# A gated-linear-attention layer: query-times-state products in plain fp32, a backward state kept decayed, gates computed in two halves

## The chip, the core and the metric

The program runs on one core of one Trainium2 chip. A core has five engines with a queue of their own each: TensorE (PE; its weight loads are shown apart as PEld), VectorE (DVE), ScalarE (ACT), GpSimd (POOL) and SyncE (SP), which here issues every DMA. Each engine takes its instructions in the order in which the program holds them, so one that waits holds up what stands behind it on its engine. The metric is the device time of one execution in microseconds (us); lower is better.

## What is computed

One layer of a transformer trunk over 2048 latent tokens and 256 context tokens: a modulated norm, a bidirectional gated linear attention (GLA), a residual, and a SwiGLU feed-forward part (FFN). What matters here is the scan. Per head, with a decay `g` for each channel and token, a state `s` (128 x 256) runs over the tokens:

```
def step(s, inp):
    qc, kc, vc, gc = inp
    b = cumsum(gc, axis=1);  b_end = b[:, -1]
    q_dec = qc * exp(b)
    scores = where(causal, q_dec @ (kc * exp(-b)).T, 0)
    o = scores @ vc + q_dec @ s
    s = exp(b_end) * s + (kc * exp(b_end - b)).T @ vc

o_f = scan(q, k, v, g_f);  o_b = flip(scan(flip(q), flip(k), flip(v), flip(g_b)))
y = (head_rms_norm(o_f + o_b) * silu(r)) @ w_out          # then residual, norm, FFN
g = log_sigmoid(glr @ w_gate + b_gate) / 16
```

The context tokens are scanned first, and their last states start both scans of the latent tokens.

## The kernel before

The latent tokens are worked in 4 groups of 512 tokens (`g`), each of 4 chunks of 128 tokens (`c`; 16 chunks in all, `gc`). There are three stages in time.

**First stage** (to about 820 us). For each group a list of 24 units (`proj_units`) projects k, v with the gate inputs (`proj_vg`, `proj_v`), q and r. Between the units the main loop puts the four steps `s0` to `s3` of each chunk (`gla_stages`), from unit 16 of a group into the next group's units; the last group's chunks lie closer. All matmuls of the projections, and most of GLA, are split: an fp32 operand becomes a high and a low part in the format fp32r (`split`: a cast, and a subtraction on DVE), and `mm3` makes high x high, high x low and low x high, three matmuls in place of one.
- `s0` loads k, q, v of a chunk. For every second chunk it also computes the gates of the pair, in both directions (`gates(0, cp)`, then `gates(1, cp)`): 4 small matmuls each (`pre`), three activations for each half on ACT (L342 to L344), a subtraction (L345, `gcs`) and a running sum (L347, `cs`) for each half on DVE, a middle value (L350) and one pass over the whole (L351).
- `s1` forms the decayed keys `ek` and queries `eq`, and splits v.
- `s2` makes the scores `sc`, the transposed keys `kt`, and the splits. For the forward state it takes `Tf` times the decay `fz`, split into `shi` (ACT, L418) and `slo` (DVE, L419), and the split of the query (`qhi`, `qlo`).
- `s3` makes the state's increments `U` for both directions. The forward one is added into `Tf` (L441); the backward one is copied out (L446) and stored to DRAM as `ub_d`. Then `o` = scores times v (one `mm3`) plus query times state (a second `mm3`), stored as `op_d`.

`proj_vg` leaves the gate inputs in PSUM; DVE takes them out in small steps (`gs` L291 and L292, `glt` L293 to L295) before PE may use that PSUM buffer again.

**Second stage** (about 820 to 1112 us). The chunks are gone through backwards (`back`), five steps each, software-pipelined over neighbouring chunks. `b0` loads `ub`, the decayed backward query `qb`, `op` and r. POOL multiplies `qb` by the chunk's decay `fb` (L650), ACT and DVE split the state `Tb` (`shi`, `slo`) and the query (`qhi`, `qlo`), and DVE updates the state, `Tb` = `Tb` x `fb` + `ub` (L653). `b1` makes query times state with `mm3` and adds it to `op` (L670), then squares on ACT, a power on POOL (`rh`, L82) and a scaling on DVE (`on`, L676). `b2` transposes and multiplies by silu(r) (`rt`, `ohi`, `olo`), `b3` multiplies by the output weights (`py`, 48 matmuls), `b4` scales (`ry` on POOL, L724 on DVE), adds the residual on POOL (L726, `y`), stores it (L727) and normalises it. SP issues the stores and the loads of later chunks in one queue.

**Third stage** (from about 1112 us). The FFN, in a seven-product scheme of split matmuls (L924, L1047). The change does not touch it.

The code's order is not the engines' order: when the program is built, a scheduler places the instructions on each engine by what it expects to be ready. Buffers are pools with a fixed count (`bufs`); a tile that takes a buffer again waits for the last reader.

Of the kernel before, what the change touches and what calls it, by code (L numbers as in the profile page):

```python
# [7 lines left out]
F32 = mybir.dt.float32  # L8
# [26 lines left out]
def trunk(ctx, tc, x, cx, modw, cols, rows, consts, wqkr, wv, wvg, wgate, wout, w1, w2, out):  # L35
# [271 lines left out]
    pair = {}  # L307

    def gla_stages(g, i, c, first):
# [3 lines left out]

        def gtile(shape, name):
            return psg.tile(shape, F32, name=name, tag="ga", bufs=4)

        def s0():
# [10 lines left out]
            e["cs"] = [t[:, c % 2:2 * H:2, :] for t in pair["cs"]]  # L328
            e["lnDf"] = pair["lnDf"][:, c % 2]

        def gates(z, cp):
            flat = lambda t: t.rearrange("p n t -> p (n t)")
            cs = gp.tile([128, 2 * H, 129], F32, name=f"cs{z}", tag=f"cs{z}", bufs=1)
            for hh in range(2):
                pre = gtile([128, 2, 256], "pre")
                for h2 in range(2):
                    h = 2 * hh + h2
                    nc.tensor.matmul(out=pre[:, h2, :], lhsT=wg[z][:, 128 * h:128 * h + 128],
                                     rhs=glrS[i][:, 256 * cp:256 * cp + 256], start=True, stop=True)
                pre = pre.rearrange("p h (c t) -> p (h c) t", c=2)  # L340
                ab = gp.tile([128, 4, 128], F32, name="ab", tag="ab", bufs=2)
                nc.scalar.activation(out=ab, in_=pre, func=AF.Abs)  # L342
                nc.scalar.activation(out=ab, in_=ab, func=AF.Exp, scale=-1.0)
                nc.scalar.activation(out=ab, in_=ab, func=AF.Ln, bias=1.0)  # L344
                nc.vector.scalar_tensor_tensor(out=gcs[:, :, 1:129], in0=pre, scalar=0.0, in1=ab,  # L345
                                               op0=ALU.min, op1=ALU.subtract)
                nc.vector.tensor_tensor_scan(out=flat(cs[:, 4 * hh:4 * hh + 4, :]), data0=flat(rst), data1=flat(gcs),  # L347
                                             initial=0.0, op0=ALU.mult, op1=ALU.add)
            mid = gp.tile([128, 2 * H, 1], F32, name="mid", tag="mid", bufs=2)
            nc.vector.tensor_scalar_mul(out=mid, in0=cs[:, :, 64:65], scalar1=1.0 / 16)  # L350
            nc.vector.scalar_tensor_tensor(out=cs, in0=cs, scalar=1.0 / 16, in1=mid.to_broadcast([128, 2 * H, 129]),  # L351
                                           op0=ALU.mult, op1=ALU.subtract)
            lnD = (pair["lnDf"] if z == 0 else lnDb[:, gc:gc + 2]).rearrange("p c h j -> p h c j")
            nc.gpsimd.tensor_copy(out=lnD[:, :, :, z], in_=mid.rearrange("p (h c) o -> p h (c o)", c=2))
            nc.gpsimd.tensor_copy(out=lnD[:, :, :, 1 - z], in_=cs[:, :, 128:129].rearrange("p (h c) o -> p h (c o)", c=2))
            return cs

        def s1():
            e["ks"], e["qs"] = [], []
            for z in range(2):  # L360
# [14 lines left out]
                if z == 0:  # L375
                    if prev["lnDf"] is not None:
                        fz = gp.tile([128, H], F32, name="fz", tag="fz", bufs=2)
                        nc.vector.tensor_add(out=fz, in0=prev["lnDf"][:, :, 1], in1=lnD[:, :, 0])
                        nc.scalar.activation(out=fz, in_=fz, func=AF.Exp)
                        e["fz"] = fz  # L380
                    prev["lnDf"] = lnD
            e["vhi"] = gp.tile([128, D], F32R, name="vhi", tag="vhi", bufs=1)
# [3 lines left out]
        def s2():  # L386
# [19 lines left out]
            if not is_ctx:  # L406
# [756 lines left out]
```

## Time and profile before

| | |
|---|---|
| median of 3 runs | 2427.31 us (2424.38 to 2429.68) |
| the profiled execution | 2426.05 us |
| its span | 2424.3 us |
| PE busy | 2313.9 us (95%) |
| DVE, ACT, POOL busy | 1644.8, 1083.0, 220.2 us |
| mean granted clock of TensorE | 0.978 |

The span runs from the first to the last instruction of the one profiled execution. A busy PE has a matmul in flight; the granted clock tells at which share of full speed it runs, and it takes two levels, 1.00 (2.4 GHz) and 0.50 (1.2 GHz). Time can thus be lost in two ways on PE: idle before an instruction, and half speed for some microseconds after.

### The profile page before, as it was taken

Reading aid. Unit: us, or ns where it says so; the run is one execution under the profiler, and the core shown is the slowest. Engines: PE = TensorE matmul, PEld = TensorE weight load, DVE = VectorE, ACT = ScalarE, POOL = GpSimd, SP = SyncE. Lnnn points to the kernel's source line nnn. Section 1 sums busy time; section 2 is a strip of 40 time slices with the busy share of each in tenths; the row PEclk is TensorE's granted clock in tenths of the full one; section 3 lists DMA queues with packets and bytes.
Section 4 is the critical chain, followed back from the end, with each engine's and each line's share of the span. In section 5 each row is a group of like instructions: output and inputs, shape, how many; then the busy total and the mean of one; then the engine's idle time right before and its main releaser. Section 6 shows DMA issues by size and latency. Waiting matters only on the chain.

```text
span 2424.3 us, 32896 instructions
## 1 busy us (share of the span) xinstructions
PE 2313.9 (95%) x11686; PEld 1952.2 (81%) x11686; DVE 1644.8 (68%) x2628; ACT 1083.0 (45%) x1930; POOL 220.2 (9%) x290
## 2 busy tenths in 40 slices
PE   8999999999999899787899999999999989999998
PEld 4898898898898777676788888888888868888887
DVE  6756668667669788776777766776565647567554
ACT  3524535435546454434433333543333326555552
POOL 1100001001001144652000000000000000001001
PEclk9999999999999999998999999999999989999999
DMA  8755367476455676657878523543233238559655
GB/s 301 230 197 176 130 211 263 159 230 205 140 199 186 218 243 228 207 190 265 276 255 268 178 96 111 191 137 109 92 109 105 92 113 293 193 184 325 212 182 175
DMA packets 229193, 465.07 MB, mean 192 GB/s; under 512 B 22562, under 2 KB 66210, under 8 KB 229028
## 3 DMA queue, kind: packets, MB, share of 16 engines
q1 hardware_dynamic: 229028, 462.96, 56.5%
q8 instruction: 92, 1.51, 0.3%
q14 instruction: 73, 0.60, 0.1%
HBM read 331.79 MB, written 131.08 MB: 191 GB/s over the span
## 4 chain that ended last, share of the span: by engine, by line
PE 52%; DMA 1%; DVE 0%; SPq 0%; ACT 0%; issue 0%; POOLq 0%; POOL 0%; ACTq 0%
PE X L924 19%; PE X L1047 10%; PE Z L924 10%; PE W L1047 7%; PE Y L924 5%; DMA wraw<-w 0%; DMA T<-T_d 0%; DMA T_d<-hf 0%; DVE sa L957 0%; DVE hf L754 0%; DVE y L1028 0%; SPq L879 0%; DVE a L947 0%; DVE bl L754 0%; DVE t L754 0%
## 5 line engine op out<-in xcount | busy, mean ns | idle before, releaser
L924 PE MATMUL X<-T,whl 128*128 128x512 f32 x2112 | 495.7, 390 | 8.2 <-ACT whl L906 7.1
L924 PEld LDWEIGHTS X<-T,whl 128*128 128x128 f32 x2112 | 396.6, 188 | 91.5 <-ACT whl L906 7.5
L924 PE MATMUL Z<-T,whl 128*128 128x512 f32 x1056 | 255.9, 391 | 9.9 <-ACT T L834 9.9
L1047 PE MATMUL X<-wr,ar 128*128 128x512 f32 x1056 | 243.6, 392 | 11.1 <-ACT wr L1011 11.1
L1047 PEld LDWEIGHTS X<-wr,ar 128*128 128x128 f32 x1056 | 200.0, 190 | 53.7 <-ACT wr L1011 11.5
L924 PEld LDWEIGHTS Z<-T,whl 128*128 128x128 f32 x1056 | 199.2, 189 | 52.3 <-ACT T L834 10.3
L86 PE MATMUL pj<-hhi,whi 128*128 128x512 f32 (+1 forms) x544 | 211.4, 390 | 1.8 <-DVE hhi L75 1.1
L87 PE MATMUL pj<-hlo,whi 128*128 128x512 f32 (+1 forms) x544 | 210.7, 388 | 0.0
L88 PE MATMUL pj<-hhi,wlo 128*128 128x512 f32 (+1 forms) x544 | 210.2, 387 | 0.0
L73 ACT CAST whi<-wf 128x1024 fp32r<-128x1024 f32 x104 | 109.1, 1049 | 213.4 <-PE pj L87 77.4
L1001 DVE TENSOR_TENSOR ar<-ar 128x512 fp32r<-128x512 f32 x154 | 106.2, 691 | 136.0 <-ACT ar L1000 135.1
L76 DVE TENSOR_TENSOR wlo<-wf,whi 128x1024 fp32r<-128x1024 f32 x104 | 126.7, 1222 | 83.0 <-ACT whi L73 72.4
L1047 PE MATMUL W<-wr,ar 128*128 128x512 f32 x792 | 180.5, 389 | 0.0
L1047 PEld LDWEIGHTS W<-wr,ar 128*128 128x128 f32 x792 | 148.6, 188 | 30.9
L1000 ACT CAST ar<-ar 128x512 fp32r<-128x512 f32 x154 | 95.4, 621 | 156.0 <-DMA ar<-S_d 103.7
L86 PE MATMUL pj<-whi,hhi 128*128 128x256 f32 x432 | 124.2, 287 | 5.7 <-DVE gs L292 4.9
L924 PE MATMUL Y<-T,whl 128*128 128x512 f32 x528 | 127.7, 390 | 0.0
L87 PE MATMUL pj<-wlo,hhi 128*128 128x256 f32 x432 | 123.3, 285 | 3.1 <-DVE wlo L76 3.1
L88 PE MATMUL pj<-whi,hlo 128*128 128x256 f32 x432 | 122.8, 284 | 0.0
L86 PEld LDWEIGHTS pj<-hhi,whi 128*128 128x128 f32 x544 | 102.9, 190 | 21.2 <-DVE hhi L75 1.3
L87 PEld LDWEIGHTS pj<-hlo,whi 128*128 128x128 f32 x544 | 103.1, 190 | 20.7 <-DVE hlo L76 1.8
L88 PEld LDWEIGHTS pj<-hhi,wlo 128*128 128x128 f32 x544 | 103.0, 189 | 19.6
(237 smaller groups left out, 4528.1 us busy)
## 6 DMA issues: line engine op xcount, KB each, us to landing
ar<-S_d SPq DMA_DIRECT2D x154, 256.0 KB, 2.8
wf<-wqkr SPq DMA_DIRECT2D x68, 512.0 KB, 4.1
wg<-w SPq DMA_DIRECT2D x44, 512.0 KB, 3.7
wu<-w SPq DMA_DIRECT2D x88, 256.0 KB, 2.6
S_d<-sa SPq DMA_DIRECT2D x88, 256.0 KB, 2.0
wr<-W_d SPq DMA_DIRECT2D x88, 256.0 KB, 2.9
wf<-wv SPq DMA_DIRECT2D x36, 512.0 KB, 4.5
wl<-w SPq DMA_DIRECT2D x66, 256.0 KB, 3.7
```

The source lines that it names most:

```text
L73: nc.scalar.copy(out=hi, in_=src)
L76: nc.vector.tensor_sub(out=lo, in0=src, in1=hi.bitcast(F32))
L86: nc.tensor.matmul(out=ps, lhsT=ahi, rhs=bhi, start=start, stop=False)
L87: nc.tensor.matmul(out=ps, lhsT=ahi, rhs=blo, start=False, stop=False)
L88: nc.tensor.matmul(out=ps, lhsT=alo, rhs=bhi, start=False, stop=stop)
L924: nc.tensor.matmul(out=ps, lhsT=w[:, a, ks], rhs=t[:, k, b, :], start=first and k == 0 and n == 0, stop=k == 3 and n == 2, skip_group_chec ...
L1000: nc.scalar.copy(out=t[:, 0, :], in_=raw)
L1001: nc.vector.tensor_sub(out=t[:, 1, :], in0=raw, in1=t[:, 0, :].bitcast(F32))
L1047: nc.tensor.matmul(out=po[j], lhsT=a[:, x, 128 * j:128 * j + 128], rhs=w[:, z, :], start=first and fp == 0 and n == 0, stop=fp == NFP - 1 ...
```

## The change

Three things are changed.
1. Query times state is one plain fp32 matmul per head, in the first stage (`eq` times `ts`, where `ts` is the decayed forward state, written by ACT alone) and in the second (`qb` times `E`). The splits of query and state, and `mm3`, are gone there. `Tf` is now `ts` + `U`, an addition for two heads at once.
2. The second stage keeps the state already decayed: `E` = decayed `Tb`, and the next `E` is `E` x `fb[gc-1]` + `ub`. So that this holds, `ub` is multiplied by `fb[gc-1]` as ACT copies it out of PSUM, one copy for each head; `fb` is computed for each chunk in `s1` in place of once between the stages. POOL's multiplication of `qb` is gone. Chunk 0 needs no `ub`: its backward `U` and the load are left out.
3. The gates of a pair are computed in two calls. The forward half of the second pair of a group comes with chunk 1, and that of the next group's first pair with chunk 3 (for groups 0 and 1); the backward half stays with the pair's first chunk. The last group's first pair is still computed in one go.

```
+    def gates(g, cp, z):
+        d = pairs.setdefault((g, cp), {})
+        if z in d:
+            return
...
+        cs = gp.tile([128, 2 * H, 129], F32, name=f"cs{z}", tag=f"cs{z}", bufs=2)
...
+    def put_fb(gc, ln1):
+        nc.vector.tensor_add(out=fb[:, gc, :], in0=ln1, in1=lnDb[:, gc, :, 0])
+        x = nc.scalar.activation(out=fb[:, gc, :], in_=fb[:, gc, :], func=AF.Exp)
+        last["exp"] = getattr(x, "ins", x)
...
             if c % 2 == 0:
-                pair["lnDf"] = gp.tile([128, 2, H, 2], F32, name="lnDf", tag="lnDf", bufs=2)
-                pair["cs"] = [gates(z, c // 2) for z in range(2)]
...
+                for z in range(2):
+                    gates(g, c // 2, z)
+                pair["now"] = pairs.pop((g, c // 2))
+            elif is_ctx:
+                pass
+            elif c == 1:
+                gates(g, 1, 0)
+            elif g in (0, 1):
+                gates(g + 1, 0, 0)
...
-                e["qhi"] = gp.tile([128, H, 128], F32R, name="qhi", tag="qhi", bufs=1)
-                e["qlo"] = gp.tile([128, H, 128], F32R, name="qlo", tag="qlo", bufs=1)
-                split(e["qs"][0], e["qhi"], e["qlo"], "dve")
-                e["shi"] = gp.tile([128, H, DV], F32R, name="shi", tag="shi", bufs=1)
-                e["slo"] = gp.tile([128, H, DV], F32R, name="slo", tag="slo", bufs=1)
+                e["ts"] = gp.tile([128, H, DV], F32, name="ts", tag="ts", bufs=1)
                 for h in range(H):
-                    f = e["fz"][:, h:h + 1]
-                    nc.scalar.activation(out=e["shi"][:, h, :], in_=Tf[:, h, :], func=AF.Copy, scale=f)
-                    nc.vector.scalar_tensor_tensor(out=e["slo"][:, h, :], in0=Tf[:, h, :], scalar=f,
-                                                   in1=e["shi"][:, h, :].bitcast(F32), op0=ALU.mult, op1=ALU.subtract)
+                    nc.scalar.activation(out=e["ts"][:, h, :], in_=Tf[:, h, :], func=AF.Copy, scale=e["fz"][:, h:h + 1])
...
                 khi, klo = e["kt"][z]
+                if z == 1 and gc == 0:
+                    break
...
+                        elif not is_ctx:
+                            nc.vector.tensor_add(out=Tf[:, hs, :], in0=e["ts"][:, hs, :], in1=U)
...
                     else:
-                        nc.scalar.copy(out=ub[:, hs, :], in_=U)
+                        for h2 in range(2):
+                            h = 2 * hh + h2
+                            nc.scalar.activation(out=ub[:, h, :], in_=U[:, h2, :], func=AF.Copy, scale=fb[:, gc - 1, h:h + 1])
...
-                    mm3(o[:, h2, :], e["qhi"][:, h, :], e["qlo"][:, h, :], e["shi"][:, h, :], e["slo"][:, h, :], False, True)
+                    nc.tensor.matmul(out=o[:, h2, :], lhsT=e["qs"][0][:, h, :], rhs=e["ts"][:, h, :], start=False, stop=True)
...
-            nc.gpsimd.tensor_tensor(out=qb, in0=qb, in1=fb[:, gc, :].unsqueeze(2).to_broadcast([128, H, 128]), op=ALU.mult)
-            split(Tb, shi, slo)
-            for h in range(H):
-                nc.vector.scalar_tensor_tensor(out=Tb[:, h, :], in0=Tb[:, h, :], scalar=fb[:, gc, h:h + 1], in1=ub[:, h, :],
-                                               op0=ALU.mult, op1=ALU.add)
...
-            split(qb, qhi, qlo)
-            e["q"], e["s"] = (qhi, qlo), (shi, slo)
...
+            e["q"], e["s"] = qb, E[0]
+            if gc:
+                nxt = sp.tile([128, H, DV], F32, name="E", tag="E", bufs=3)
+                for h in range(H):
+                    nc.vector.scalar_tensor_tensor(out=nxt[:, h, :], in0=E[0][:, h, :], scalar=fb[:, gc - 1, h:h + 1],
+                                                   in1=ub[:, h, :], op0=ALU.mult, op1=ALU.add)
+                E[0] = nxt
...
-                    mm3(o[:, h2, :], qhi[:, h, :], qlo[:, h, :], shi[:, h, :], slo[:, h, :], True, True)
+                    nc.tensor.matmul(out=o[:, h2, :], lhsT=e["q"][:, h, :], rhs=e["s"][:, h, :], start=True, stop=True)
```

The scheduler makes new orders of it. The first place is DVE at the gate inputs of group 1, when the gates of group 0's second pair are due; before, DVE holds, up to the second `gs`:

```order
L347 SCALAR_TENSOR_TENSOR cs_2854<-rst,gcs 128x516
L378 TENSOR_TENSOR fz<-lnDf 128x4
L76 TENSOR_TENSOR wlo<-wf,whi 128x1024
L345 SCALAR_TENSOR_TENSOR gcs<-pre,ab 128x4x128
L236 COPY stg<-pj 128x256
L347 SCALAR_TENSOR_TENSOR cs_2854<-rst,gcs 128x516
L291 COPY gs<-pj 128x32
L350 TENSOR_SCALAR mid<-cs_2854 128x8
L368 TENSOR_TENSOR ek<-kc,ek 128x512
L351 SCALAR_TENSOR_TENSOR cs_2854<-cs_2854,mid 128x1032
L292 TENSOR_TENSOR gs<-pj,gs 128x32
L291 COPY gs<-pj 128x32
```

Here `cs_2854` is the backward half, and the forward half (the same six instructions) stands just ahead of these rows. In the changed kernel the same place on DVE reads:

```order
L350 TENSOR_TENSOR fb<-lnDb 128x4
L76 TENSOR_TENSOR wlo<-wf,whi 128x1024
L391 TENSOR_TENSOR ek<-kc,ek 128x512
L236 COPY stg<-pj 128x256
L291 COPY gs<-pj 128x32
L394 SCALAR_TENSOR_TENSOR eq<-qc,eq 128x512
L292 TENSOR_TENSOR gs<-pj,gs 128x32
L350 TENSOR_TENSOR fb<-lnDb 128x4
L293 CAST glt_363<-gs 128x32
L294 CAST glt_363<-gs 128x32
L295 TENSOR_TENSOR glt_363<-gs,glt_363 128x32
L291 COPY gs<-pj 128x32
```

Only one half stands ahead of these rows now; no step of the gates is left between or just ahead of the two `gs`, and the other half stands one chunk earlier in the queue.

The second place is POOL in the second stage, over one chunk; before, its queue reads:

```order
L726 TENSOR_TENSOR y_9484<-y_9484,xt_9634 128x1024
L650 TENSOR_TENSOR qb_10093<-qb_10093,fb 128x512
L80 TENSOR_SCALAR mh<-ssh 128x4
L82 TENSOR_TENSOR rh<-mh,nhalf 128x4
L720 TENSOR_TENSOR sst<-ss_9655 128x1
L80 TENSOR_SCALAR my<-sst 128x1
L82 TENSOR_TENSOR ry<-my,nhalf 128x1
L650 TENSOR_TENSOR qb_10239<-qb_10239,fb 128x512
L726 TENSOR_TENSOR y_9654<-y_9654,xt_9804 128x1024
```

The same chunk's piece of the changed kernel on POOL:

```order
L753 TENSOR_TENSOR y_9122<-y_9122,xt_9256 128x1024
L80 TENSOR_SCALAR mh<-ssh 128x4
L82 TENSOR_TENSOR rh<-mh,nhalf 128x4
L747 TENSOR_TENSOR sst<-ss_9277 128x1
L80 TENSOR_SCALAR my<-sst 128x1
L82 TENSOR_TENSOR ry<-my,nhalf 128x1
L753 TENSOR_TENSOR y_9276<-y_9276,xt_9410 128x1024
```

The multiplications of `qb`, which wait for a load, are gone from ahead of `mh` and of `y`; the rest of POOL's work stands as it stood.

## Rows read from the trace of the kernel before

**Rows 1.** Page, part 1: busy us, share of span, instructions.

```profile
PE 2313.9 (95%) x11686; PEld 1952.2 (81%) x11686; DVE 1644.8 (68%) x2628; ACT 1083.0 (45%) x1930; POOL 220.2 (9%) x290
```

**Rows 2.** Windows by stage: us; PE, PEld, DVE, ACT, POOL busy; granted clock; DMA.

```profile
100.00:820.00 720.00, 693.40 (x4356) 625.59 (x4356) 515.70 (x839) 345.78 (x558) 40.67 (x53) 0.98 0.57 190
820.00:1112.00 292.00, 256.78 (x1244) 209.78 (x1243) 219.88 (x372) 131.35 (x305) 135.30 (x151) 0.95 0.66 224
...
1300.00:1981.00 681.00, 681.00 (x3006) 563.88 (x3005) 437.32 (x679) 257.39 (x451) 0.00 (x0) 1.00 0.37 124
```

**Rows 3.** Waits of PE in 100 to 820: us in total, times, longest.

```profile
PE pj L86 <- DVE gs L292: 4.9, 2, 4.4
PE sc L392 <- DVE eq L371: 4.1, 3, 2.7
PE pj L287 <- DVE gs L291: 3.4, 1, 3.4
PE pj L529 <- DVE gs L291: 3.4, 1, 3.4
```

**Rows 4.** Timeline of DVE before the stall that ends at 288.65: start, us.

```profile
284.30 0.68 DVE L345 SCALAR_TENSOR_TENSOR gcs<-pre,ab 128x512 f32<-128x512 f32 x1
...
285.23 1.22 DVE L347 TENSOR_TENSOR_SCAN cs<-rst,gcs 128x516 f32<-128x516 f32 x1
...
287.18 1.23 DVE L351 SCALAR_TENSOR_TENSOR cs<-cs,mid 128x1032 f32<-128x1032 f32 x1
```

**Rows 5.** Windows at the half clock after two stalls, columns as in Rows 2.

```profile
287.70:294.40 6.70, 5.75 (x24) 5.78 (x25) 4.71 (x16) 1.15 (x2) 0.20 (x1) 0.50 0.37 115
...
731.40:741.60 10.20, 7.73 (x33) 7.12 (x34) 10.18 (x23) 5.00 (x10) 2.90 (x3) 0.50 0.21 67
```

**Rows 6.** PE timeline (start, us), and one tile's durations (ns min/median/max).

```profile
219.18 0.28 PE L86 MATMUL U<-vhi,khi 128*128 128x256 f32 x1
219.30 0.28 PE L87 MATMUL U<-vlo,khi 128*128 128x256 f32 x1
...
211.04 1.95 PE L392 MATMUL sc<-eq,ek 128*128 128x128 f32 x16
...
329.50 1.02 PE L520 MATMUL pj<-acc,ones 128*128 128x512 f32 x2
...
L520 PE MATMUL pj<-acc,ones x8: 590/592/697, 329.5 to 549.0; 128*128 128x512 f32 x8
```

**Rows 7.** Groups of instructions: busy us, mean ns; then idle before them.

```profile
L653 DVE SCALAR_TENSOR_TENSOR Tb<-Tb,fb,ub 128x256 f32<-128x256 f32 x64 | 45.3, 755 | 2.5 <-DMA ub<-ub_d 2.4
...
L419 DVE SCALAR_TENSOR_TENSOR slo<-Tf,fz,shi 128x256 fp32r<-128x256 f32 x64 | 28.4, 478 | 0.0
...
L76 DVE TENSOR_TENSOR slo<-Tb,shi 128x1024 fp32r<-128x1024 f32 x16 | 19.5, 1216 | 4.2 <-ACT shi L73 4.2
...
L76 DVE TENSOR_TENSOR qlo<-qb,qhi 128x512 fp32r<-128x512 f32 x16 | 13.1, 822 | 1.6 <-ACT qhi L73 1.6
```

**Rows 8.** Waits of PE in 820 to 1112, columns as in Rows 3.

```profile
PE o L86 <- ACT hf L103: 9.2, 4, 3.6
PE py L86 <- DVE ohi L75: 6.3, 3, 2.4
PE tp L695 <- DVE on L676: 6.3, 4, 3.2
...
PE o L86 <- ACT qhi L73: 2.6, 1, 2.6
```

**Rows 9.** Waits of POOL and SP from 820; POOL and DVE timelines near 950.

```profile
POOL qb L650 <- DMA qb<-qb_d: 67.8, 10, 39.1
...
SPq L727 <- POOL y L726: 71.2, 14, 9.5
...
949.74 1.04 POOL L650 TENSOR_TENSOR qb<-qb,fb 128x512 f32<-128x512 f32 x1 [8.14 <-DMA qb<-qb_d]
...
952.20 1.15 DVE L676 TENSOR_SCALAR on<-op,rh 128x256 f32<-128x256 f32 x4 [3.15 <-POOL rh L82]
```

More of the change, by code (lines that the diff above doesn't have):

```diff
@@ L306, in trunk, with gtile @@
     prev = {"lnDf": None}
-    pair = {}
+    pair, pairs = {}, {}
+    def gtile(shape, name):
+        return psg.tile(shape, F32, name=name, tag="ga", bufs=4)
+    def gates(g, cp, z):
+        d = pairs.setdefault((g, cp), {})
+        if z in d:
+            return
+        i = 1 if g == NG else g % 2
+        gc = NC_ if g == NG else 4 * g + 2 * cp
+        if z == 0:
+            d["lnDf"] = gp.tile([128, 2, H, 2], F32, name="lnDf", tag="lnDf", bufs=3)
+        flat = lambda t: t.rearrange("p n t -> p (n t)")
+        cs = gp.tile([128, 2 * H, 129], F32, name=f"cs{z}", tag=f"cs{z}", bufs=2)
+        for hh in range(2):
+            pre = gtile([128, 2, 256], "pre")
+            for h2 in range(2):
+                h = 2 * hh + h2
+                nc.tensor.matmul(out=pre[:, h2, :], lhsT=wg[z][:, 128 * h:128 * h + 128],
+                                 rhs=glrS[i][:, 256 * cp:256 * cp + 256], start=True, stop=True)
+            pre = pre.rearrange("p h (c t) -> p (h c) t", c=2)
+            ab = gp.tile([128, 4, 128], F32, name="ab", tag="ab", bufs=2)
+            nc.scalar.activation(out=ab, in_=pre, func=AF.Abs)
+            nc.scalar.activation(out=ab, in_=ab, func=AF.Exp, scale=-1.0)
+            nc.scalar.activation(out=ab, in_=ab, func=AF.Ln, bias=1.0)
+            nc.vector.scalar_tensor_tensor(out=gcs[:, :, 1:129], in0=pre, scalar=0.0, in1=ab,
+                                           op0=ALU.min, op1=ALU.subtract)
+            nc.vector.tensor_tensor_scan(out=flat(cs[:, 4 * hh:4 * hh + 4, :]), data0=flat(rst), data1=flat(gcs),
+                                         initial=0.0, op0=ALU.mult, op1=ALU.add)
+        mid = gp.tile([128, 2 * H, 1], F32, name="mid", tag="mid", bufs=2)
+        nc.vector.tensor_scalar_mul(out=mid, in0=cs[:, :, 64:65], scalar1=1.0 / 16)
+        nc.vector.scalar_tensor_tensor(out=cs, in0=cs, scalar=1.0 / 16, in1=mid.to_broadcast([128, 2 * H, 129]),
+                                       op0=ALU.mult, op1=ALU.subtract)
+        lnD = (d["lnDf"] if z == 0 else lnDb[:, gc:gc + 2]).rearrange("p c h j -> p h c j")
+        nc.gpsimd.tensor_copy(out=lnD[:, :, :, z], in_=mid.rearrange("p (h c) o -> p h (c o)", c=2))
+        nc.gpsimd.tensor_copy(out=lnD[:, :, :, 1 - z], in_=cs[:, :, 128:129].rearrange("p (h c) o -> p h (c o)", c=2))
+        d[z] = cs
@@ L309, in gla_stages @@
+    last = {}
+    def put_fb(gc, ln1):
+        nc.vector.tensor_add(out=fb[:, gc, :], in0=ln1, in1=lnDb[:, gc, :, 0])
+        x = nc.scalar.activation(out=fb[:, gc, :], in_=fb[:, gc, :], func=AF.Exp)
+        last["exp"] = getattr(x, "ins", x)
     def gla_stages(g, i, c, first):
@@ L325, in s0 @@
             if c % 2 == 0:
-                pair["lnDf"] = gp.tile([128, 2, H, 2], F32, name="lnDf", tag="lnDf", bufs=2)
-                pair["cs"] = [gates(z, c // 2) for z in range(2)]
[L328 to L356, printed above, removed]
@@ L358, in s1 @@
+                for z in range(2):
[7 more added lines that the diff above has]
+                gates(g + 1, 0, 0)
+            now = pair["now"]
+            e["cs"] = [now[z][:, c % 2:2 * H:2, :] for z in range(2)]
+            e["lnDf"] = now["lnDf"][:, c % 2]
         def s1():
@@ L381, in s1 @@
                     prev["lnDf"] = lnD
+                elif not is_ctx and gc:
+                    put_fb(gc - 1, lnDb[:, gc, :, 1])
+                    if gc == NC_ - 1:
+                        put_fb(gc, lnDb[:, NC_, :, 1])
             e["vhi"] = gp.tile([128, D], F32R, name="vhi", tag="vhi", bufs=1)
@@ L444, in s3 @@
                         nc.scalar.copy(out=Tb[:, hs, :], in_=U)
-                    else:
-                        nc.scalar.copy(out=ub[:, hs, :], in_=U)
+                    elif is_ctx:
+                        nc.scalar.copy(out=ub[:, hs, :], in_=U)
+                    else:
+                        for h2 in range(2):
+                            h = 2 * hh + h2
+                            nc.scalar.activation(out=ub[:, h, :], in_=U[:, h2, :], func=AF.Copy, scale=fb[:, gc - 1, h:h + 1])
                 if z == 1:
@@ L566, in trunk @@
         wait = 0
-        last = g == NG - 1
-        if last:
+        is_last = g == NG - 1
+        if is_last:
             tail = pu[-3:]
@@ L572, in trunk @@
             u()
-            if not last and i + 1 == nq:
+            if not is_last and i + 1 == nq:
                 for c in range(4):
@@ L579, in trunk @@
                 mu.pop(0)()
-            if last:
+            if is_last:
                 if i + 1 >= LAST_AT:
@@ L601, in trunk @@
     p1.close()
-    nc.vector.tensor_add(out=fb[:, 0:NC_ - 1, :], in0=lnDb[:, 1:NC_, :, 1], in1=lnDb[:, 0:NC_ - 1, :, 0])
-    nc.vector.tensor_add(out=fb[:, NC_ - 1, :], in0=lnDb[:, NC_, :, 1], in1=lnDb[:, NC_ - 1, :, 0])
-    fbf = fb.rearrange("p c h -> p (c h)")
-    last_exp = nc.scalar.activation(out=fbf, in_=fbf, func=AF.Exp)
-    last_exp = getattr(last_exp, "ins", last_exp)
+    last_exp = last["exp"]
     p2 = ExitStack()
@@ L622, in load_wo @@
             split(w, *wo[k])
+    E = {}
     def back(gc):
```

19 lines of the change are left out of this document (9 added, 10 removed).

## Prediction

> **What bounds the kernel now.** The page's first part comes first: PE is busy for 95% of the span, and no other engine comes near it [rows 1]. So the kernel is bound by PE, and a change pays only if it makes PE's own work shorter or takes away time in which PE stands still or runs at half speed. The windows by stage tell where such time is [rows 2]. The FFN's long middle has none: PE is busy 681.00 of 681 us at full clock. The first stage idles 720 - 693.4 = 26.6 us, and its granted clock of 0.98 means that some 2% of 720, 14 us, goes to half speed. The second stage is much worse for its length: 292 - 256.8 = 35.2 us idle, and at 0.95 another 5% of 292, 15 us. Together 41 us in the first and 50 us in the second are the most that can be won; between them the stages hold every instruction that the change touches.
>
> Next I read what PE waits for. In the first stage the largest waits are for DVE: for `gs`, the emptying of the gate inputs' PSUM (4.9, 3.4 and 3.4 us), and for `eq` (4.1) [rows 3]. At the stall that ends at 288.65 DVE is not idle; it is working off the gates of a pair: one half takes two L345 at 0.68, two L347 at 1.22, one L351 at 1.23 and a short L350, about 5.1 us, and two halves stand one behind the other with the `gs` among them [rows 4]. Each long stall is followed by a stretch at the lower of TensorE's two levels, 6.7 us behind that one, 10.2 us behind the one near 732 [rows 5]; at half speed half of that is lost, so a stall of 3.4 us costs some 3.4 + 3.4.
>
> **Part 1a, the fp32 products: a cost on PE.** A split product of 128 x 256 is three matmuls that start 0.12 us apart [rows 6], 3 x 0.12 = 0.36 us per head. The trace has no fp32 matmul of 256 columns, but two neighbours. Each shows as two instructions per matmul. The 16 `sc` instructions of 128 columns cover 1.95 us, which with a last one of about 0.28 is (1.95 - 0.28) / 15 = 0.111 us each; of the two `pj` instructions of 512 columns the second begins 1.02 - 0.59 = 0.43 us after the first [rows 6]. In between, 256 columns come to 0.111 + (0.43 - 0.111) x 128 / 384 = 0.217 us, so a product is 2 x 0.217 = 0.434 us, 0.074 more than before. There are 16 chunks x 4 heads = 64 such products in each stage: +4.7 us in each. Bounds: 0.22 per head (the narrower neighbour's price), which is -9 us for each stage, and 0.86 (the wider one's), +32. The value is linear between two rows, so I hold it for good.
>
> The Trainium skill, "FP8 and Floating Point Precision", section TensorE Precision Notes, says that true fp32 takes four passes through the array. Taken as four for three at the split product's own spacing, that is 0.48 us a head, +7.7 us in each stage, an estimate that would put the total 6 us higher; the two neighbours above, measured, are cheaper than that.
>
> Chunk 0's backward `U` goes: 4 heads x 3 matmuls x 0.12 = -1.4 us on PE.
>
> **Part 1b, the splits: a relief of DVE and ACT.** In the first stage each chunk loses four L419 of 0.478 on DVE [rows 7], 1.9 us, besides the two splits of the query; DVE, busy 515.7 of 720 [rows 2], loses at least 64 x 0.478 = 31 us. None of the waits in [rows 3] names these instructions; they only shorten the queue in front of the ones that are named. I count nothing for that by itself beyond 2 us for the small waits left over, and up to 5 as a bound.
>
> In the second stage DVE loses `slo` (19.5 us) and `qlo` (13.1) out of 219.9 [rows 2, 7], ACT the two casts, POOL the 16 multiplications of `qb`. The four updates of the state (L653) stay as they are. Their mean is 755 ns where L419, of the same shape and beside a quiet POOL, takes 478 [rows 7], so they run against something in this stage; with a third engine's work gone some of that should go too, but I put no sum on it.
>
> **Part 2, the decayed state.** POOL no longer waits for the load of `qb`. This is the larger half of the change in the second stage: POOL stood at that load 10 times for 67.8 us in the trace [rows 9], 39.1 of it once before the stage began to turn. Behind it in POOL's queue stand `mh` and `rh`, for which DVE's `on` waits, and `y`, for whose store SP waits 71.2 us, with the loads of the next chunks behind that store [rows 9]. Near 950 it can be followed: POOL gets `qb` after 8.14 us of waiting, only then `rh`, and DVE starts `on` after 3.15 us of idling [rows 9]. PE's waits in the stage are of this kind: for `on`, for `ohi`, for a PSUM buffer that `hf` on ACT holds [rows 8]. What the change moves to `s1` and `s3` (16 tiny adds and exponentials, two copies more per chunk on ACT, busy 345.8 of 720 [rows 2]) lies beside matmuls; if that cover failed it would be under 1 us a chunk.
>
> How much of the second stage's 50 us goes? At least the wait that ends on a removed instruction, `qhi`, 2.6 us [rows 8], and a unit of clock with it: 3 us. At most some 45, all but the wind-up. DVE loses 32.6 of 219.9 us, 15%, and POOL its longest wait, while the chain op, square, power, `on`, transposes, `ohi` and the order L726, L727, loads remain. I take 27, a little over half, nearer to the upper end since most of PE's waits sit behind the two queues that are emptied. Net of the products: -27 + 4.7 = -22.3.
>
> **Part 3, the gates in halves.** By the order, the two `gs` at group 1 have one half of 5.1 us ahead of them in place of two [rows 4]; the same holds at group 2. The stall of 3.4 us at each then shrinks to about nothing, and with it the 6.7 us at half speed: 2 x (3.4 + 3.4) = 13.6, of which I take 12. The wait for `eq` (the longest 2.7 [rows 3], near 397) stands behind the first gates of group 1, of which one half is gone: 3 with its clock. The stall near 732 is group 3's first pair, which is still computed in one go, and DVE's order there is the same as before: 4.4 us of wait and 10.2 us at half speed [rows 3, 5] stay. The half that is moved needs 5.1 us of DVE somewhere else, six times in all; I put it at nothing, since DVE is idle for 204 of the 720 us [rows 2] and gets 31 us freer, and since PE there works from loaded weights. If it were not covered it would make a stall of up to 3.4 us at each of the six, +20 us.
>
> **The sum.** First stage: +4.7 - 1.4 - 2 - 12 - 3 = -13.7. Second: -22.3. Together -36.0 against the profiled execution's 2426.05, so 2390.0 us. That execution lies 1.3 us under the median of the runs, less than the runs differ among themselves, and I leave it there.
>
> **The rivals.** (a) *Only the first stage gains.* The second stage stays bound by the round trip of ACT, POOL and DVE and by SP's store of `y`, which the change leaves: only 3 us of its 50 go. For it: SP's wait for `y` is the longest in the stage, and the four L653 are not touched. Time: 2426.05 - 13.7 - 3 + 4.7 = 2414. (b) *The second stage comes close to PE's own work.* 45 of 50 us go: 2426.05 - 13.7 - 45 + 4.7 = 2372. For it: DVE's load falls well under PE's. (c) *PE takes over POOL's wait.* The product now reads `qb` as it lands, with nothing in front; the loads still queue on SP behind the store of `y`. If each of 14 chunks waited what POOL waited apart from its long one, (67.8 - 39.1) / 9 = 3.2 us [rows 9], and lost 1.7 at half clock, it would be 14 x 4.9 = +69 in place of the 27 won: 2426.05 - 13.7 + 4.7 + 69 = 2486. It ends slower from (13.7 - 4.7) / 14 = 0.6 us a chunk on, if nothing else were won there. Against it: before, `qb` landed at 949.74 and PE's product followed only after a multiplication, a cast and a subtraction, which now leave some 2.5 us of slack. (d) *The gains are small and the moved halves stall PE*, -13.7 + 20 in the first stage and rival (a)'s +1.7 in the second: 2434, slower as well; part of it, a few us of new stalls, would end near no change. That the change does not do what it says is excluded for the order at groups 1 and 2, which the built program shows.
>
> **How the numbers follow.** My forecast, both stages gain as summed, 2390 with its own bounds from 2378 to 2403: 0.52. Rival (a), 2403 to 2421: 0.20. Rival (b), 2358 to 2378: 0.16. (c) and (d) together 0.07, of which 0.06 are slower; no change 0.05 with what is left. The range reaches up over most of (a) and down over most of (b): 2365 to 2417. A measurement of this kernel tells some 0.2%, 4.9 us, from no change. Faster by more than that (under 2422): 0.89; within it: 0.05; slower: 0.06.
>
> **What would show it.** Right: the windows of 100 to 820 lose the half-clock stretches near 288 and 479 and keep the one near 732; an `o` product shows as two instructions some 0.217 us apart; POOL has no wait for `qb`; the second stage gets some 22 us shorter, with DVE under 190 us busy in it; the FFN keeps its 681 us piece. Wrong: PE waiting for a DMA of `qb`; new waits of PE for `wlo` or `gs` where the moved half stands; PE's waits in the second stage unchanged in kind and sum, which is (a); or products at 0.48 us or more a head.

## The result and the profile after

The changed kernel takes 2387.48 us (median of 4 runs, 2384.77 to 2391.16) against 2428.49 (4 runs) of the kernel before: a ratio of 0.9834, 95% interval 0.9813 to 0.9854. It is faster by 1.7%, and the forecast of 2390.0 was 2.5 us too high. The forecast stood on a profiled execution of 2426.05 us; of the change itself it foretold 36.0 us, and by the medians 41.0 were measured. The profiled execution took 2384.77 us, 41.3 less than that of before.

The page's first part of the changed kernel (busy us, share of the span, instructions), beside [rows 1]:

```profile
PE 2302.0 (97%) x11546; PEld 1939.9 (81%) x11546; DVE 1557.7 (65%) x2478; ACT 1068.8 (45%) x1947; POOL 186.6 (8%) x274
```

PE is busy for 12 us less (half speed counts as busy); the other 29 of the 41 us are time in which it stood still. To see where, the span is cut at two events that both kernels have: the start of the last matmul into `U` (end of the first stage) and the start of the FFN's first matmul into `X`. The windows of the kernel before, cut there (us; PE, PEld, DVE, ACT, POOL busy with instructions; granted clock; DMA share; GB/s):

```profile
100.00:818.00 718.00, 691.40 (x4339) 623.59 (x4339) 514.75 (x839) 344.75 (x556) 40.67 (x53) 0.98 0.57 191
818.00:1124.40 306.40, 264.10 (x1284) 215.77 (x1282) 232.35 (x387) 140.38 (x324) 141.24 (x157) 0.94 0.66 225
1124.40:2424.30 1299.90, 1270.25 (x5576) 1049.45 (x5576) 832.08 (x1281) 548.68 (x977) 25.72 (x50) 0.99 0.53 179
```

and of the changed kernel:

```profile
100.00:805.80 705.80, 688.30 (x4271) 618.86 (x4270) 475.10 (x726) 350.63 (x599) 37.58 (x53) 0.99 0.57 193
805.80:1085.80 280.00, 257.62 (x1216) 209.36 (x1214) 185.43 (x351) 119.66 (x299) 110.80 (x141) 0.98 0.72 244
1085.80:2383.00 1297.20, 1268.95 (x5576) 1048.52 (x5576) 832.42 (x1281) 549.55 (x977) 26.82 (x50) 0.99 0.53 179
```

The first stage is 12.2 us shorter (forecast: 13.7), the second 26.4 (forecast: 22.3), and 2.7 us are the FFN's, which has the same instructions; a second profile of the same kernel has 1298.8 us there, so part of that is chance. In the second stage PE idles 22.4 us in place of 42.3, and its clock went from 0.94 to 0.98.

PE's waits in the first stage of the changed kernel (total us, times, longest), beside [rows 3]:

```profile
PE pj L86 <- DVE gs L292: 4.9, 2, 4.3
PE tp L102 <- ACT hf L103: 3.1, 3, 2.3
PE pj L87 <- DVE wlo L76: 2.3, 2, 1.7
```

The two `gs` waits of 3.4 us at groups 1 and 2 are gone and `eq` has left the head of the list; the 4.3 us at group 3 stand, as forecast, with 10.3 us at half clock behind them. That window of the changed kernel, beside the second one of [rows 5]:

```profile
719.40:729.70 10.30, 7.98 (x34) 7.37 (x35) 10.28 (x25) 4.94 (x11) 2.75 (x3) 0.50 0.22 71
```

What DVE does in the changed kernel where the stall of [rows 4] was (start, us): one half of the gates ends at 279.4, and no step of it stands between the two `gs`.

```profile
278.13 1.23 DVE L339 SCALAR_TENSOR_TENSOR cs<-cs,mid 128x1032 f32<-128x1032 f32 x1
...
281.64 0.18 DVE L291 COPY gs<-pj 128x32 f32<-128x32 f32 x1
281.74 0.68 DVE L394 SCALAR_TENSOR_TENSOR eq<-qc,eq 128x512 f32<-128x512 f32 x1
282.34 0.18 DVE L292 TENSOR_TENSOR gs<-pj,gs 128x32 f32<-128x32 f32 x1
```

The price of an fp32 product can now be read directly. PE's timeline in the changed kernel, one head of the first stage (start, us), and below it one chunk of the second stage:

```profile
261.87 0.59 PE L494 MATMUL o<-ts,eq 128*128 128x256 f32 x2
262.12 0.47 PE L86 MATMUL o<-vhi,phi 128*128 128x256 f32 x1
262.42 0.28 PE L87 MATMUL o<-vlo,phi 128*128 128x256 f32 x1
262.54 0.29 PE L88 MATMUL o<-vhi,plo 128*128 128x256 f32 x1
262.67 0.60 PE L494 MATMUL o<-ts,eq 128*128 128x256 f32 x2
...
870.43 1.89 PE L695 MATMUL o<-E,qb 128*128 128x256 f32 x8
871.97 0.58 PE L86 MATMUL py<-wo_hi,ohi 128*128 128x512 f32 x1
```

From head to head it is 262.67 - 261.87 = 0.80 us, and the median over the first stage is 0.787; before it was 0.713, so a product costs 0.074 more. Eight instructions of the second stage begin within 1.54 us, 0.216 apart by the median.

PE's waits in the second stage of the changed kernel (total us, times, longest), beside [rows 8]:

```profile
PE X L951 <- ACT whl L933: 7.1, 1, 7.1
PE tp L722 <- DVE on L703: 5.6, 4, 2.5
PE o L695 <- ACT hf L103: 4.6, 2, 3.2
...
PE o L695 <- DMA qb<-qb_d: 0.8, 1, 0.8
```

The first row is the wait of the FFN's first product at the stage's end, 7.1 us before as well. The others are of the old kinds, but fewer. The new wait of rival (c), for the load of `qb`, came once and took 0.8 us.

### The profile page after: what moved, and what is told of

Same layout as the page of the kernel before. It is cut to its first block, busy times and chain, and to the rows that moved or that the text cites. A ratio compares the mean times of both kernels' runs of the same rounds, so it can differ in the third digit from the quotient of the medians.

```text
span 2383.0 us, 32426 instructions
## 1 busy us (share of the span) xinstructions
PE 2302.0 (97%) x11546; PEld 1939.9 (81%) x11546; DVE 1557.7 (65%) x2478; ACT 1068.8 (45%) x1947; POOL 186.6 (8%) x274
## 4 chain that ended last, share of the span: by engine, by line
PE 52%; DMA 0%; DVE 0%; SPq 0%; ACT 0%; issue 0%; POOLq 0%; POOL 0%; ACTq 0%
PE X L951 20%; PE Z L951 10%; PE X L1074 10%; PE W L1074 8%; PE Y L951 5%; DMA wraw<-w 0%; DMA T<-T_d 0%; DMA T_d<-hf 0%; DVE sa L984 0%; DVE bl L781 0%; DVE y L1055 0%; SPq L906 0%; DVE t L781 0%; DVE hf L781 0%; DVE a L974 0%
## 5 line engine op out<-in xcount | busy, mean ns | idle before, releaser
L76 DVE TENSOR_TENSOR wlo<-wf,whi 128x1024 fp32r<-128x1024 f32 x104 | 126.8, 1220 | 86.5 <-ACT whi L73 81.0
```

The costliest lines, as they stand in the source:

```text
L76: nc.vector.tensor_sub(out=lo, in0=src, in1=hi.bitcast(F32))
```

## The experiments

### Is each stage's gain its own?

Two kernels each put one stage back. *second_old* has the changed first stage and the old second stage; *first_old* the other way round. Beside them the changed kernel ran once more.

> The changed kernel once more, beside the three that follow, so that each stands against it under the same conditions. Both theories: 2387 us, 2383 to 2392.

Measured: 2388.6 us, ratio 0.9835 (0.982 to 0.9851).

```
 second_old:
-            e["q"], e["s"] = qb, E[0]
...
+            nc.gpsimd.tensor_tensor(out=qb, in0=qb, in1=fb[:, gc, :]..., op=ALU.mult)
+            split(Tb, shi, slo)
...
+            split(qb, qhi, qlo)
```

> The changed kernel with the whole second stage as it was: POOL multiplies the query by the chunk's decay, query and state are split, the product is three matmuls, the state is not kept decayed. The first stage keeps its changes. If the two stages' gains are independent, as the prediction sums them, the second stage gets its 27 us back and the first keeps its 12: 2415 us, 2410 to 2420. If the second stage is faster only because it is entered earlier or in another order, it stays fast: under 2400.

Measured: 2409.22 us, ratio 0.9923 (0.9905 to 0.9941), 20.6 us more than the changed kernel by the medians, which is 0.8 us under the range expected, and 26.6 by the two profiles. Its second stage is 305.0 us long (before: 306.4).

```
 first_old:
-            elif c == 1:
-                gates(g, 1, 0)
-            elif g in (0, 1):
-                gates(g + 1, 0, 0)
...
-                    nc.tensor.matmul(out=o[:, h2, :], lhsT=e["qs"][0][:, h, :], rhs=e["ts"][:, h, :], ...)
+                    mm3(o[:, h2, :], e["qhi"][:, h, :], e["qlo"][:, h, :], e["shi"][:, h, :], e["slo"][:, h, :], False, True)
```

> The first stage as before (gates of a pair in one go, query and forward state split, three matmuls, the state's update in one step), the second stage as changed. If the first stage's gain is its own, 12 us come back: 2400 us, 2396 to 2404. If the second stage gives less when it is entered from the old first stage: over 2406.

Measured: 2397.38 us, ratio 0.9894 (0.9873 to 0.9915); it ran on a second chip, as did *gates_whole*, *pool_pow* and *early3_ydve*, on which the kernel before had 2423.49, so the ratios are to be compared: 0.0059 more than the changed kernel, 14 us. Its first stage ends at 818.9 (before: 818.0), its second is 280.6 us long (changed: 280.0). Each stage's gain is its own, and the sum of the prediction may be taken apart by stages.

A window is read from one execution, so it scatters. The changed first stage, with the same order on every engine, ends between 803.4 and 808.8 us in five profiles (the changed kernel's two and those of the three kernels *pool_dummy*, *pool_free* and *pool_pow* below). The changed second stage scatters less: it is 278.2 to 280.9 us long in five (the changed kernel's two, *first_old*, *gates_whole*, *early3*).

### First stage: the halves or the splits?

*gates_whole* undoes only the halves; the fp32 products stay.

```
-            elif is_ctx:
-                pass
-            elif c == 1:
-                gates(g, 1, 0)
-            elif g in (0, 1):
-                gates(g + 1, 0, 0)
```

> Only the gates' halves are undone: both halves of a pair are computed with the pair's first chunk; the plain fp32 products stay in both stages. The prediction's theory (the halves take the stalls of 3.4 us near 288 and 479 away, with 6.8 us of half clock behind each, and shorten the wait near 397): those stalls are back, 13 to 17 us come back, 2400 to 2405. The rival (the 31 us that the splits took of DVE have removed the stalls already): 2386 to 2391, without them.

Measured: 2401.48 us, ratio 0.9912 (0.9893 to 0.9931) on the second chip, 0.0077 or some 19 us more than the changed kernel. Its first stage ends at 825.2. The windows of the first stage, *gates_whole* and then *first_old*:

```profile
100.00:825.20 725.20, 697.38 (x4274) 627.23 (x4273) 472.29 (x728) 354.19 (x600) 31.71 (x54) 0.98 0.56 188
```

```profile
100.00:818.90 718.90, 690.79 (x4329) 623.32 (x4328) 516.13 (x853) 351.40 (x597) 33.97 (x53) 0.98 0.56 190
```

PE's waits in *gates_whole* (total, times, longest):

```profile
PE pj L86 <- DVE gs L292: 5.5, 2, 4.4
PE pj L551 <- DVE gs L291: 3.4, 1, 3.4
PE pj L287 <- DVE gs L291: 3.4, 1, 3.4
...
PE sc L413 <- DVE mid L338: 2.1, 1, 2.1
```

The two stalls of 3.4 us are back to the digit, though DVE is as free as in the changed kernel: 472 us busy in the stage, against 475 there and 516 in *first_old*. So the halves, not the freed DVE, take them away. They pay twice: PE idles 27.8 us here and 17.5 in the changed kernel, and it is busy 9 us longer with the same matmuls, at a granted clock of 0.98 in place of 0.99.

From *first_old* this kernel differs by the forward products and splits, the addition into `Tf`, and a second buffer for the gates' `cs`. Its first stage ends 6.3 us later (4.1 by the medians); 4.7 us of that are the products by their forecast. PE idles the same in both, 27.8 and 28.1 us, so no relief by the freed DVE is to be seen, but 2 us of it would be lost in the scatter.

### The stall that the forecast left in place

*early3* computes the last group's first pair in halves too, the forward half two projection units earlier.

```
+            if is_last and i + 1 == 10:
+                gates(g, 0, 0)
```

> The changed kernel in which the last group's first pair is computed in two halves too: the forward half two projection units earlier. The prediction left the stall near 732 (4.4 us of waiting, 10.2 us at half clock) in place because that pair is still computed in one go. If that is its cause, the wait shrinks to under 1.5 us, the half clock behind it goes or gets shorter, and the time falls by 5 to 9 us: 2378 to 2383. If the stall is set by something else (the gate inputs' other steps, the decayed keys), no change: 2385 to 2391.

Measured: 2382.96 us, ratio 0.9817 (0.9802 to 0.9831). The window of the stall (columns as above) runs at full clock, with twice the matmuls:

```profile
719.00:729.70 10.70, 8.67 (x67) 7.84 (x67) 10.70 (x25) 6.04 (x11) 1.32 (x2) 1.00 0.60 197
```

and the whole first stage, with PE's waits for `Tf` and what is left of the one for `gs`:

```profile
100.00:802.70 702.70, 685.15 (x4270) 615.70 (x4269) 475.82 (x725) 349.96 (x598) 37.88 (x53) 1.00 0.58 194
```

```profile
PE o L86 <- DVE Tf L461: 3.2, 2, 1.9
...
PE pj L287 <- DVE gs L292: 0.4, 1, 0.4
```

The gate inputs' wait at group 3 had the named cause. The gain is small: 4 to 6 us by ratios and medians, at or under the lower end of what was expected, and by the ratios' intervals it is not clear of the changed kernel. By the prediction's way of counting a wait of 4.4 us and 10.2 us at half clock come to 9.5. PE idles as long as before, 17.5 us in the stage in both kernels, since other waits have grown (for `Tf`, 0.8 us in the changed kernel); what the trace shows as gained is the half clock.

### Second stage: POOL's wait or the splits?

The prediction named POOL's stand at the load of `qb` as the larger half of the gain. *mult_back* undoes the decayed state alone, *splits_back* the plain product alone.

```
 mult_back:
+            nc.gpsimd.tensor_tensor(out=qb, in0=qb, in1=fb[:, gc, :]..., op=ALU.mult)
...
-                    ... scalar=fb[:, gc - 1, h:h + 1],
+                    ... scalar=fb[:, gc, h:h + 1],
 splits_back:
+            split(Tb, shi, slo)
...
+            split(qb, qhi, qlo)
+            e["q"], e["s"] = (qhi, qlo), (shi, slo)
```

> Only the decayed state is undone: the product stays one plain fp32 matmul per head, but POOL multiplies the query by the decay again, and the state's update uses the chunk's own decay, with no scale on the copies in the first stage. The prediction's theory (POOL standing at the load of the query, with the head norm and the residual queued behind it, is the larger half of the second stage's gain): 14 to 25 us come back, 2402 to 2412 us, with POOL waiting for that load for 40 us or more. The rival (the gain comes from the work that left DVE and ACT, the splits): under 8 us come back, 2388 to 2395.

> The opposite half of the second stage is undone: the state is kept decayed and POOL multiplies nothing, but query and state are split again on ACT and DVE and the product is three matmuls of 0.12 us per head. The prediction's theory: DVE gets its 33 us of splits back, but the queue of POOL is free, so under 13 us come back, 2388 to 2400. The rival: the splits were the wait that counted, 15 to 28 us come back, 2403 to 2415.

Measured: *mult_back* 2403.18 us, ratio 0.9896 (0.988 to 0.9911); *splits_back* 2404.06, ratio 0.9902 (0.9882 to 0.9923). Either half takes back about 15 us: the first is just inside the range of the prediction's theory (and POOL waits 86.5 us for the load in it), the second inside that of the rival. The windows of the second stage, *mult_back*:

```profile
810.50:1103.20 292.70, 262.05 (x1216) 211.26 (x1214) 190.43 (x352) 117.44 (x293) 129.35 (x157) 0.97 0.69 234
```

and *splits_back*:

```profile
809.70:1103.20 293.50, 261.82 (x1279) 215.06 (x1277) 221.50 (x383) 142.23 (x327) 118.24 (x141) 0.95 0.69 232
```

From 305.0 us with both in place either removal alone leads to about 293, and both to 279: two halves of equal size that add up, the splits' one net of the dearer products. "The larger half" is refuted. (Besides the edit, *mult_back* has plain copies of `ub` in the first stage, and *splits_back*, like *second_old*, two buffers for `qb`; the first stages of both end at 810.5 and 809.7 us, later than in the changed kernel, which is in the medians and not in the windows.)

### Which property of the multiplication costs?

Three kernels add one operation of POOL per chunk to the changed kernel, into a tile that nothing reads. The order of PE, DVE, ACT and SP stays the changed kernel's in all three; POOL's queue has the 16 extra operations and is otherwise as it was. The scheduler puts them at the same places in *pool_free* and *pool_pow*, and at others in *pool_dummy*.

```
 pool_dummy:
+            nc.gpsimd.tensor_tensor(out=junk, in0=qb, in1=fb[:, gc, :]..., op=ALU.mult)
 pool_free:
+            nc.gpsimd.tensor_tensor(out=junk, in0=e["s"][:, :, 0:128], in1=fb[:, gc, :]..., op=ALU.mult)
 pool_pow:
+            nc.gpsimd.tensor_tensor(out=junk, in0=fb[:, gc, :], in1=e["s"][:, :, 0], op=ALU.pow)
```

> The changed kernel in which POOL multiplies the loaded backward query by the decay as before, but into a scratch tile that nothing reads; PE takes the query as it lands. So POOL's queue is as long and waits for the same load, while the product has no step in front of it. If the price of the multiplication is what stands behind it on POOL (head norm, residual), the time is that of the kernel with the multiplication put back: 12 to 15 us more than the changed kernel, 2400 to 2404. If the price is the step in the product's own path, 0 to 4 us more: 2387 to 2392.

> As the kernel with the unread multiplication, but POOL's extra operation reads the state, which is on the chip, in place of the loaded query, so it takes the same 1.0 us of POOL sixteen times and waits for no load of its own. If the wait for the load is what counts: 0 to 5 us more than the changed kernel, 2387 to 2393. If it is POOL's time or the run beside DVE: as the unread multiplication, 2398 to 2404.

> As the kernel in which POOL's extra operation reads the state, at the same sixteen places of POOL's queue and with the same wait for the state's update, but the operation is a power of 128 x 4 elements (the head norm's own power of that shape takes POOL 1.06 us) in place of a product of 128 x 512 (1.04 us). All other engines keep the changed kernel's order. If POOL's time and its queue cost the 12 us of the second stage: as there, 2394 to 2402 us. If the cost comes from POOL and DVE streaming beside each other (DVE's busy time in that stage grew by 11 us with the same instructions): 2386 to 2391, with DVE's busy time in the stage within 3 us of the changed kernel's 185.

Measured: *pool_dummy* 2397.69 us, ratio 0.9873 (0.9857 to 0.989); *pool_free* 2395.0, ratio 0.9868 (0.9854 to 0.9883); *pool_pow* 2396.88, ratio 0.9894 (0.9873 to 0.9915) on the second chip. The first two lie between the two ranges that were expected of them, so their times decide nothing; the third lies in the range for POOL's time. What POOL waited for in front of the extra operation, from 800 on, in *pool_dummy*:

```profile
POOL junk L681 <- DMA qb<-qb_d: 82.4, 8, 45.1
```

and in *pool_free*:

```profile
POOL junk L681 <- issue: 40.6, 1, 40.6
POOL junk L681 <- DVE E L686: 16.4, 5, 5.0
```

The second stage of *pool_free* and then of *pool_pow*:

```profile
808.80:1098.90 290.10, 259.21 (x1216) 208.82 (x1214) 195.38 (x353) 119.54 (x299) 126.88 (x157) 0.98 0.70 236
```

```profile
803.40:1093.50 290.10, 261.14 (x1215) 212.22 (x1213) 184.54 (x353) 119.41 (x299) 127.22 (x157) 0.96 0.69 236
```

The stage is 290.2, 290.1 and 290.1 us long in the three, against 278.2 to 280.9 in the five profiles without the extra operation. DVE, with the same instructions in the same order, is busy 195 us in *pool_free* and 184.5 in *pool_pow*: the same length, so POOL and DVE streaming beside each other at this operation is not what costs. What costs shows on POOL's timeline (start, us). In eight of the 16 chunks these two kernels have the extra operation right behind `rh`, ahead of `sst`, `ry` and `y`. One such chunk in the changed kernel:

```profile
896.80 1.02 POOL L82 TENSOR_TENSOR rh<-mh,nhalf 128x4 f32<-128x4 f32 x1
897.78 0.20 POOL L747 TENSOR_TENSOR sst<-ss 128x1 f32<-128x1 f32 x1
...
912.19 1.02 POOL L82 TENSOR_TENSOR rh<-mh,nhalf 128x4 f32<-128x4 f32 x1
```

and the same chunk in *pool_free*:

```profile
903.04 1.02 POOL L82 TENSOR_TENSOR rh<-mh,nhalf 128x4 f32<-128x4 f32 x1
904.02 1.04 POOL L681 TENSOR_TENSOR junk<-E,fb 128x512 f32<-128x512 f32 x1
905.02 0.24 POOL L750 TENSOR_TENSOR sst<-ss 128x1 f32<-128x1 f32 x1
...
919.33 1.02 POOL L82 TENSOR_TENSOR rh<-mh,nhalf 128x4 f32<-128x4 f32 x1
```

From one `rh` to the next it is 15.4 us in the first and 16.3 in the second: the chunk is longer by what the operation takes. *pool_dummy* is as long by another way. There POOL stands at the load of `qb` with `mh` and `rh` behind it, and DVE's `on` waits, as the prediction had read it near 950 [rows 9]:

```profile
931.72 1.04 POOL L681 TENSOR_TENSOR junk<-qb,fb 128x512 f32<-128x512 f32 x1 [7.07 <-DMA qb<-qb_d]
...
933.12 1.02 POOL L82 TENSOR_TENSOR rh<-mh,nhalf 128x4 f32<-128x4 f32 x1
```

```profile
934.18 1.14 DVE L705 TENSOR_SCALAR on<-op,rh 128x256 f32<-128x256 f32 x4 [4.54 <-POOL rh L82]
```

This one step, from `rh` to `rh`, is 15.6 us against 10.9 in the changed kernel, half of what the extra operation costs the stage. So a wait for the load does cost where `mh` stands behind it, but little of the 82 us does: 45.1 of them lie ahead of the first chunk. And a microsecond of POOL costs where it lies in the chunk's chain. The three stages are equally long, but not for one reason. The product's own step, which *mult_back* has in addition, costs at most 2.5 us more.

### The splits, unread

*split_dummy* lets ACT and DVE split as before, while PE keeps the plain product.

```
+            js = sp.tile([128, H, DV], F32R, name="js", tag="js", bufs=1)
+            split(E[0], js, js)
...
+            split(qb, jq, jq)
```

> The changed kernel in which ACT and DVE split the backward query and state as before, but into tiles that nothing reads; PE keeps the plain fp32 product. If the splits cost by the time they take of ACT and DVE (33 us of DVE): 12 to 16 us more than the changed kernel, 2400 to 2405. If they cost by standing between the load and the product: 0 to 5 us more, 2387 to 2393.

Measured: 2411.83 us, ratio 0.9939 (0.9924 to 0.9954), above both ranges; the stage is 302.6 us long. The splits cost even where no product waits for them. That this costs 9 us more than in *splits_back* is not explained by the theory: the scratch tiles have one buffer each, so that ACT has to wait for DVE and DVE for ACT, and DVE's order differs from both; which of these costs was not tried. The run shows that latency is not needed for the price, and it does not measure the price.

### The next microsecond of POOL

If POOL's time in the round trip counts, its largest piece is the residual addition `y` (L753), 2.45 us a chunk. *early3_ydve* is *early3* with that addition on DVE.

```
-            (nc.vector if gc == 0 else nc.gpsimd).tensor_tensor(out=y, in0=y, in1=xt, op=ALU.add)
+            nc.vector.tensor_tensor(out=y, in0=y, in1=xt, op=ALU.add)
```

> The kernel with the last group's gates in halves too, in which the residual addition of the second stage (POOL, 2.45 us for each of 15 chunks) is DVE's. If POOL's streaming beside DVE and its queue are what holds the second stage: faster by 3 to 10 us than that kernel's 2383, 2373 to 2380. If DVE's own load holds it: DVE gets about 18 us more, slower by 3 to 10 us, 2386 to 2393.

Measured: 2370.88 us, ratio 0.9786 (0.9766 to 0.9806) on the second chip, the fastest kernel here, faster than the changed one and under the range expected. Its second stage:

```profile
802.00:1068.40 266.40, 252.32 (x1215) 207.43 (x1213) 190.68 (x367) 119.56 (x299) 76.54 (x126) 0.99 0.75 257
```

266.4 us against *early3*'s 280.9, and against 280.6 and 280.2 in *first_old* and *gates_whole* on the same chip. By the ratios of the whole time it is 0.0031 or 7.5 us less than *early3*, with intervals that overlap; the 14 us are the profiles'. DVE has 15 additions more (1.22 us each) and is busy only 5 us longer; POOL has lost 34 us. PE's two longest waits there (total, times, longest), 5.1 and 4.2 us in *early3*, are shorter:

```profile
PE tp L724 <- DVE on L705: 3.2, 3, 1.3
PE o L697 <- ACT hf L103: 2.9, 2, 1.5
```

Three things may give the 14 us, and they were not tried apart: the shorter addition itself (1.22 us in place of 2.45 ahead of `xh`), the free queue for `rh` and `rb`, and DVE's other work, which takes some 14 us less where no `y` of POOL runs beside it (15 x 1.22 more, 5 measured).

## Why the prediction was right

**What bounds the kernel, and where.** Right. The matmuls hardly changed; the gain is stalls and half clock of the two stages, and the FFN kept its length but for 2.7 us.

**The fp32 products.** Right to the digit: 0.074 us more for each; between the rows for 128 and 512 columns [rows 6] a straight line held at 256. The Trainium skill, "FP8 and Floating Point Precision", section TensorE Precision Notes, counts four passes for true fp32; four times the spacing of 0.12 between the matmuls of a split product would be 0.48 us, an estimate, and the two instructions measured 2 x 0.216 = 0.43.

**The relief of the first stage's DVE.** Forecast 2 us, and none was seen: between *first_old* and *gates_whole* PE's idle time stays (28.1 and 27.8 us), and the stage gets 4.1 to 6.3 us longer where the prediction's terms give 4.7 - 2 = 2.7. None of the waits in [rows 3] ends on a split of query or state. With a scatter of 5 us in the first stage it stays open whether the term is 2 us or nothing.

**The gates' halves.** Forecast 12 + 3 = 15 us; *gates_whole* takes back some 19 by the ratios, 16 to 22 by where the stage ends. The stalls and their half clock went as read from [rows 3 to 5], and group 3's stall stayed, until *early3* removed it by the same means. The wait for `mid` (2.1 us, before as in *gates_whole*) went too and was not in the sum. The stage as a whole came out 12.2 us shorter, forecast 13.7; that one term made up for another is not shown.

**The second stage.** Forecast 27 before the products, measured 26.4 after them, so some 31. The size, "a little over half", held; the weights within it did not. The path that the prediction named is there: POOL at the load, `rh` behind it, DVE's `on` waiting for 3.15 us near 950 [rows 9] and for 4.54 in *pool_dummy*. But its waiting, 67.8 us [rows 9], stood for "the larger half", and *pool_dummy* with 82.4 us of it is no slower than *pool_free*, which waits for no load of its own. The prediction gave no price to POOL's own time, and in *pool_free* and *pool_pow* 1 us of it a chunk, where it lies in the chunk's chain, is the price. How the two shared in the kernel before was not taken apart. And the splits, which the prediction put beside it, are worth as much: 12 us alone each, 25 to 27 together.

**The rivals.** (a), the round trip stays: refuted, though the stage is still bound by it, as *early3_ydve* shows with another 14 us. (b), 45 us: not reached by this change; 22.4 us of idling are left. (c), PE waits for `qb`: one wait of 0.8 us. (d), new stalls from the moved halves: small ones at most. No wait for `wlo` or `gs` is new; PE's list gained 1.5 us ahead of a gates' matmul (`pre`, for `p`) and 3.1 us for `hf`, and whether the moved halves cause these is open. DVE's busy time in its second stage is 185 us, under the 190 named; it was 232 in the same stretch of before.

## What to carry to other kernels

The sum of an engine's waits is not a price: a wait costs where something that is needed stands behind it. Unread operations (one that waits, one that doesn't, one that streams little) tell causes apart only where they stand at the same place of the queue, so read from the trace where each one landed; here two equal times came about in different ways. A slow engine that is idle most of the time (POOL, 111 of 280 us busy) can still set a stage's length when its operations lie in each chunk's round trip. A stall of a few microseconds ahead of PE costs twice where the clock falls behind it (in *gates_whole* 10 us of standing and 9 of slower matmuls), so an order that keeps two long pieces of work from standing together can be worth more than making either shorter.

## What the runs showed of the hardware

DVE's scaling `on` takes 0.35 us, and 2.46 the one time that it starts beside POOL's `y`; the state's update takes 0.48 and up to 2.61, twice beside a `y`. The durations (ns, least, median, most) in the changed kernel:

```profile
L703 DVE TENSOR_SCALAR on<-op,rh x64: 342/349/2459, 823.8 to 1054.2; 128x256 f32<-128x256 f32 x64
L683 DVE SCALAR_TENSOR_TENSOR E<-E,fb,ub x60: 470/477/2610, 815.8 to 1008.6; 128x256 f32<-128x256 f32 x60
```

and in *early3_ydve*, where POOL does no `y`:

```profile
L705 DVE TENSOR_SCALAR on<-op,rh x64: 343/348/356, 820.0 to 1037.7; 128x256 f32<-128x256 f32 x64
L685 DVE SCALAR_TENSOR_TENSOR E<-E,fb,ub x60: 470/475/919, 812.1 to 995.8; 128x256 f32<-128x256 f32 x60
```

The updates of [rows 7], with a mean of 755 ns, ran against more: of those that took longer, three ran beside a `y`, seven beside the multiplication of `qb` and four beside POOL's subtractions for the FFN (`bl`). The Trainium skill, "SBUF — State Buffer", section Who interferes with whom, says that the two engines share one pair of ports, that the lock on it is exclusive, and that a DVE instruction with two SBUF inputs, as the update is, contends with a GpSimd instruction that reads SBUF; the traces agree (2.61 us is about the length of one `y`). What this costs a stage is shown for the extra operation alone: *pool_pow* takes its streaming away, with DVE's busy time back at 184.5 us, and the stage stays at 290.1. For `y` it is open.
